# A fused S5 and Fourier network on one core: complex products summed by TensorE, the head's elementwise work on VectorE, the chunk scan as an up and a down sweep

## The chip, the cores and the metric

The kernel runs on one core of a Trainium2 chip. The metric is the device time of one execution in microseconds (us), as the median of several runs; lower is better. The change touches the first part of the program alone, its "head".

## The reference, cut to what matters

The program applies one adaptive-norm block with an S5 mixer and a squared-ReLU MLP to 256 latent tokens of 2048 channels, and then a block of two layers (convolution and spatial gating, Fourier mixing, two gated FFNs), all in fp32. The head computes the S5 mixer up to its Gelu: for each of 128 groups of 16 channels a complex state of 64 numbers goes over the 256 context tokens and then over the 256 latent ones, once forward and once backward in time, and the real part of C times the states is the output.

```python
def s5_discretise(a_re, a_im, log_dt, b_re, b_im):
    lam = lax.complex(a_re.astype(jnp.float32), a_im.astype(jnp.float32))
    dt = jnp.exp(log_dt.astype(jnp.float32))[:, None]
    lam_bar = jnp.exp(lam * dt)
    b = lax.complex(b_re.astype(jnp.float32), b_im.astype(jnp.float32))
    b_bar = ((lam_bar - 1) / lam)[..., None] * b
    return lam_bar, b_bar

def s5_scan(u, lam_bar, b_bar, s0, reverse):
    bu = jnp.einsum('btgh,gph->btgp', u, b_bar)
    first = -1 if reverse else 0
    bu = bu.at[:, first].add(lam_bar * s0)
    a = jnp.broadcast_to(lam_bar, bu.shape)
    _, states = lax.associative_scan(_lin_rec_combine, (a, bu), axis=1, reverse=reverse)
    return states
...
    for direction in range(2):
...
        st_ctx = s5_scan(uc_ctx, lam_bar, b_bar, s0, reverse)
        s_ctx_final = st_ctx[:, 0] if reverse else st_ctx[:, -1]
        st_lat = s5_scan(uc_lat, lam_bar, b_bar, s_ctx_final, reverse)
        y_lat = y_lat + jnp.einsum('btgp,ghp->btgh', st_lat, c_mat).real
```

## The kernel before, in words

**The tiling.** The 256 tokens of each stream are cut into 32 chunks of 8 (`L = 8`, `NC_ = 32`). The 128 groups are cut into four batches of 32 (`NB = 4`, `GB = 32`), and a batch's work into steps of four groups. The partitions hold the 64 states of both directions (2 x 64), or 8 tokens times 16 channels. PW, Q, R and WP hold powers of the discretised eigenvalue: Q those that carry a token to the end of its chunk, R those that carry a chunk's first state to its tokens, WP the powers 8, 16, 32, 64 and 128 for the scan over chunks.

**The stages of a batch** are generators in `s5_batch`, one `yield` for each step:

- `m`, `modulate()`: B is loaded; Bx (difference and sum of B's two parts) and qd (difference of Q's two parts) are made, on GpSimd but for batch 0; GpSimd multiplies the inputs u by their rstd rs; VectorE applies shift and scale to u. These come from `mod_matmul`, whose weights go through SP's queue of transfers.
- `e`, `inputs()`: eight steps. In each, `build` (L390 to L407) makes X, the complex product of Q's powers and B, by three products and two additions of 128x512 elements: the first product, tX, belongs to the real and to the imaginary part and is added to both. TensorE transposes X's eight 128x128 blocks (recorded at L69) into two PSUM banks, ScalarE copies them to W1 (L469), TensorE multiplies W1 by u (L476, 16 matmuls of 64 rows and 64 columns), and ScalarE copies the result into EC (context) and EL (latent), four copies of 64 partitions each (L484 and L485), in reversed order for the backward direction.
- `s`, `scan()`: the end states of the context's 32 chunks are summed in a tree of five levels (EC, at most four states in an instruction); the result is copied to EL[:, 0] (L525); then a loop over the 31 later chunks makes EL's states one after the other. One update is `mac`, L512 to L515: two products and two additions of 64 elements for each state.
- `z`, `outputs()`: eight steps. `build` makes Z, the conjugate powers R times C, in the same way; ScalarE copies B into bm (L557); TensorE makes the kernel of each group within a chunk from bm and Z (L562, and L566 for the diagonal); ScalarE copies it to Kp (L569) and issues four transfers that lay it out as the Toeplitz tile W4 (L573); ScalarE copies the states into SN (L576 and L577); `product`, two steps later (`ZLAG`), multiplies SN by Z and u by W4 into one bank (L545) and applies Gelu (L547). After the eight steps come transposes and the casts to high and low parts, z (L595 on ScalarE, L596 on VectorE).

**Which engine.** The tables X_ENG, Z_ENG and TREE (L34 to L38) give each step's `build` and each batch's tree to VectorE ('v') or GpSimd ('p'): of the 32 X, VectorE makes 24, of the 32 Z two, of the four trees three. X and Z of GpSimd lie in slots of tag Z, X of VectorE in slots of tag X.

**What sets the order.** ORDER (L44) is a list by hand: "m0:1" is one step of batch 0's modulation, "e2+z0:4" four steps each of batch 2's chunk inputs and batch 0's outputs in turn, and it ends in "s2 e3+z1 s3 z2 z3". Within each e step some modulation matmuls of a later batch are put (MODS), within z steps some of `mod_vectors` (WORK). The whole head stands in `tc.block(schedule_with_timeline_sim=True)`, whose scheduler then places the instructions on each engine. PSUM has four banks of tag ps (transposes and chunk inputs), two of py (kernels and products) and two of ab (modulation) in the head. Behind it is the dense part, products with weights from DRAM (`Dense.block`, first matmul line L648).

Of the kernel before, what the change touches and what calls it, by code (L numbers as in the profile page):

```python
# [18 lines left out]
P = 128  # L19
# [3 lines left out]
G = 128  # L23
# [95 lines left out]
def rstd_of(nc, pool, out, ssq, n, eps, shape, nm):  # L119
    """out = (ssq / n + eps) ** -0.5, with one Newton step."""  # L120
# [10 lines left out]
def cmul(eng, tmp, out, a, b):  # L131
    """out = a * b; re and im on axis -2 of out and b; a = (re, im) views without that axis."""
# [9 lines left out]
def head(k, raw, ctx):  # L142
# [8 lines left out]
    Q = hq.tile([P, 2, L, G], F32, name="Q")  # L151
# [8 lines left out]
    with ExitStack() as bx:  # L160
# [5 lines left out]
        sp = b2.tile([P, 3, GB, 16], F32, tag="C", name="sp").rearrange("p a b c -> p (a b c)").rearrange("p (n g) -> p n g", g=G)  # L166
# [17 lines left out]
        for b in range(NB):  # L184
            for i in range(2):
                u = uT[b][:, i]
                nc.sync.dma_start(u, a["xu"][:, b, i])
                sq = b3.tile([P, 2, 4, L * 16], F32, tag="X", name=f"xq{b}_{i}", bufs=XBUFS).rearrange("p a b c -> p (a b c)")
# [37 lines left out]
        for ri in range(2):  # L226
            S.copy(Q[0:64, ri, 1:8], PW[0:64, 7:0:-1, ri])
            S.copy(Q[0:64, ri, 0], WP[0:64, 0, ri])
            S.copy(Q[64:128, ri, 0:7], PW[64:128, 1:8, ri])
            S.copy(Q[64:128, ri, 7], WP[64:128, 0, ri])  # L230

        bms = []
        for i in range(2):
            bm = pools[0].tile([P, 2, 9, 16], F32, name=f"bm{i}")
# [58 lines left out]
def mod_vectors(k, raw, pool, st, vecs):  # L293
    """Column layout of the modulation vectors 2 to 5 for the latent stream, a step of 128 rows at a time."""
# [27 lines left out]
class ModVectors:  # L322
    """Modulation vectors 3 and 5 of the latent stream, feature by feature: sums over w_mod's columns times silu(c)."""
# [8 lines left out]
    def steps(self, raw, v):  # L332
        """One step for each 128 features and half of the rows."""
# [16 lines left out]
def mod_matmul(k, raw, b, st, acc):  # L350
    """Shift and scale of 512 channels before the bias, [(vector, half of the rows, stream), channels], in eight steps for each part."""
# [25 lines left out]
def s5_batch(k, pools, act, za, b, rs, ub, Q, R, WP, dd, bms, acc, ahead, work):  # L377
    """The stages of 32 groups: modulation, chunk inputs, scan, outputs; each is a generator of its steps."""
# [7 lines left out]
    def outer(p, m, jh):  # L386
        """Views of powers [p, j, g] and of m [p, g, h], over (g, j, h) or (g, h, j)."""
        shp = [P, 4, L, 16] if jh else [P, 4, 16, L]
        return (p.rearrange("p j g -> p g j").unsqueeze(3 if jh else 2).broadcast_to(shp),
                m.unsqueeze(2 if jh else 3).broadcast_to(shp))  # L390

    def build(tag, s, pw, pd, m, conj, jh):
        """Powers times m (or their conjugates) for four groups, with three products: the first belongs to both parts."""
        c = (Z_ENG if conj else X_ENG)[b][s]
        e = Pl if c == "p" else V
        slot = "Z" if conj or c == "p" else "X"
        out = b3.tile([P, 2, 4, L * 16], F32, tag=slot, name=f"{tag}{b}_{s}", bufs=ZBUFS if slot == "Z" else XBUFS)
# [92 lines left out]
    def scan():  # L490
# [36 lines left out]
        for c in range(1, NC_):  # L527
            mac(V, EL[:, c : c + 1], EL[:, c - 1 : c], 0, 1)
            if c % 4 == 3:
                yield  # L530
# [884 lines left out]
```

## Time and profile before

| | before |
|---|---|
| median of 3 runs | 3508.19 us (3506.8 to 3509.62) |
| the profiled execution: span, which is also all that the page times of it | 3504.0 us |
| TensorE, matmuls (PE), busy | 3164.2 us, 90% |
| TensorE, weight loads (PEld), busy | 3010.3 us, 86% |
| VectorE (DVE), busy | 2224.0 us, 63% |
| ScalarE (ACT), busy | 1474.4 us, 42% |
| GpSimd (POOL), busy | 556.2 us, 16% |

The profile is of one execution; its times are in us from the start of the span, and busy time leaves out branches, semaphores and the issue of transfers. A share of the whole span is a mean over the head and the dense part, so the stretches of the head are read by themselves: as slices of a fortieth of the span each, as windows with the busy time of each engine, as groups of instructions by line and shape, and as single instructions in order of time.

### The profile page before, as it was taken

The numbers are of one execution on the slowest core, as the hardware profiler recorded it, in microseconds if no ns is written. First come the engines' busy times: TensorE is split into PE (matmuls) and PEld (weight loads), VectorE is DVE, ScalarE is ACT, GpSimd is POOL, SyncE is SP. The second block draws the span as 40 slices with busy tenths as digits, with TensorE's granted clock in tenths as the row PEclk, the third lists the DMA queues.
The fourth block names the chain that finished last, engine by engine and source line by source line (L and its number), as shares of the span: only waits on it lengthen the run. The fifth ranks groups of instructions, "written<-read, shape, count | busy, mean of one in ns | idle before, by whom it ended". The sixth has DMA issues, their size and how long they took to land.

```text
span 3504.0 us, 66511 instructions
## 1 busy us (share of the span) xinstructions
PE 3164.2 (90%) x28206; PEld 3010.3 (86%) x28206; DVE 2224.0 (63%) x2936; ACT 1474.4 (42%) x1817; POOL 556.2 (16%) x368
## 2 busy tenths in 40 slices
PE   4655635998999999989999999999999999999998
PEld 1333325998999999988899999999999999999998
DVE  8999993678556554568855555554556555555455
ACT  2435424554444444443554433433444443343343
POOL 5756563011000000027710000000000000000000
PEclk7887756999999999999999999999999999999999
DMA  6664515784777766645555656666654665666664
GB/s 213 219 202 134 157 25 160 259 264 148 236 235 232 227 188 187 187 151 162 162 161 178 186 187 184 190 187 187 187 169 139 177 187 188 187 185 190 187 187 140
DMA packets 353530, 641.80 MB, mean 183 GB/s; under 512 B 23120, under 2 KB 92496, under 8 KB 352848
## 3 DMA queue, kind: packets, MB, share of 16 engines
q1 hardware_dynamic: 331824, 620.19, 56.9%
q10 hardware_dynamic: 21408, 17.36, 2.2%
q8 instruction: 220, 3.60, 0.4%
q14 instruction: 78, 0.64, 0.0%
HBM read 626.96 MB, written 2.10 MB: 180 GB/s over the span
## 4 chain that ended last, share of the span: by engine, by line
PE 52%; DVE 1%; issue 0%; ACT 0%; POOL 0%; DVEq 0%; ACTq 0%; POOLq 0%
PE ps L648 50%; PE ps L663 1%; PE ps L1260 0%; POOL wl L620 0%; PE ps L737 0%; PE ps L1285 0%; DVE xT L1234 0%; PE ps L750 0%; PE ps L1044 0%; PE ps L1121 0%; DVE pq L1277 0%; PE ps L1039 0%; PE ps L69 0%; DVE fl L1298 0%; DVE wl L620 0%
## 5 line engine op out<-in xcount | busy, mean ns | idle before, releaser
L620 DVE TENSOR_TENSOR wl<-wr,wh 128x1024 fp32r<-128x1024 f32 x907 | 1116.0, 1233 | 1028.4 <-ACT wh L619 1028.0
L619 ACT CAST wh<-wr 128x1024 fp32r<-128x1024 f32 x976 | 1022.7, 1049 | 1498.6 <-PE ps L648 1376.2
L648 PE MATMUL ps<-f,wh 128*128 128x256 f32 x5632 | 995.7, 279 | 0.0
L648 PEld LDWEIGHTS ps<-f,wh 128*128 128x128 f32 x5632 | 860.0, 188 | 0.1
L648 PE MATMUL ps<-f,wl 128*128 128x256 f32 x2816 | 787.6, 280 | 0.0
L648 PEld LDWEIGHTS ps<-f,wl 128*128 128x128 f32 x2816 | 527.9, 187 | 0.0
L648 PE MATMUL ps<-m,wh 128*128 128x256 f32 x2048 | 366.4, 281 | 8.8 <-DVE m L930 5.7
L648 PE MATMUL ps<-hd,wh 128*128 128x256 f32 x2048 | 360.6, 280 | 0.0
L648 PEld LDWEIGHTS ps<-m,wh 128*128 128x128 f32 x2048 | 315.0, 188 | 10.9 <-DVE m L930 6.9
L648 PEld LDWEIGHTS ps<-hd,wh 128*128 128x128 f32 x2048 | 312.6, 188 | 0.0
L648 PE MATMUL ps<-m,wl 128*128 128x256 f32 x1024 | 287.3, 281 | 0.0
L648 PE MATMUL ps<-hd,wl 128*128 128x256 f32 x1024 | 286.5, 280 | 0.0
L648 PE MATMUL ps<-f1d,wh 128*128 128x256 f32 x1408 | 248.9, 280 | 0.0
L648 PE MATMUL ps<-f0d,wh 128*128 128x256 f32 x1408 | 247.9, 280 | 0.0
L648 PEld LDWEIGHTS ps<-f1d,wh 128*128 128x128 f32 x1408 | 215.1, 188 | 0.0
L648 PEld LDWEIGHTS ps<-f0d,wh 128*128 128x128 f32 x1408 | 215.0, 188 | 0.0
L648 PE MATMUL ps<-f1d,wl 128*128 128x256 f32 x704 | 197.1, 280 | 0.0
L648 PE MATMUL ps<-f0d,wl 128*128 128x256 f32 x704 | 196.9, 280 | 0.0
L648 PE MATMUL ps<-z,wh 128*128 128x256 f32 x1024 | 184.5, 282 | 9.8 <-ACT wh L619 9.8
L648 PEld LDWEIGHTS ps<-m,wl 128*128 128x128 f32 x1024 | 193.3, 189 | 0.0
L648 PEld LDWEIGHTS ps<-hd,wl 128*128 128x128 f32 x1024 | 192.5, 188 | 0.0
L620 POOL TENSOR_TENSOR wl<-wr,wh 128x1024 fp32r<-128x1024 f32 x69 | 167.7, 2440 | 113.5 <-ACT wh L619 107.7
(491 smaller groups left out, 4730.2 us busy)
## 6 DMA issues: line engine op xcount, KB each, us to landing
wr<-in_ffn_w_gate_dram SPq DMA_DIRECT2D x176, 512.0 KB, 3.7
wr<-in_ffn_w_up_dram SPq DMA_DIRECT2D x176, 512.0 KB, 3.7
wr<-in_ffn_w_down_dram SPq DMA_DIRECT2D x176, 512.0 KB, 3.7
wr<-in_w_mlp_in_dram SPq DMA_DIRECT2D x128, 512.0 KB, 3.9
wr<-in_w_mlp_out_dram SPq DMA_DIRECT2D x128, 512.0 KB, 3.9
wv<-in_w_mod_dram SPq DMA_DIRECT2D x64, 512.0 KB, 5.0
wr<-in_s_w_glu_dram SPq DMA_DIRECT2D x64, 512.0 KB, 5.2
wv<-in_w_modt_dram SPq DMA_DIRECT2D x64, 512.0 KB, 4.4
```

Source lines behind the costliest of these rows:

```text
L619: nc.scalar.copy(hi, t)
L620: self.low(n).tensor_tensor(lo, t, hi.bitcast(F32), op=ALU.subtract)
L648: nc.tensor.matmul(o, lhsT=w[:, nt * P : (nt + 1) * P], rhs=x, start=(kt == 0 and nt % 2 == 0 and i == 0), stop=(kt == nk - 1 and nt % 2 = ...
L663: nc.tensor.matmul(acc[tt], lhsT=x[:, tk], rhs=w, start=(kt == 0 and i == 0), stop=(kt == nk - 1 and i == 2))
```

## The change: what it does

1. **X and Z are three products each, and nothing is added on an engine for elementwise work.** X is a list of three tiles (Q's real part times Bx, Q's imaginary part times the sum, qd times B's imaginary part), Z one of three parts. All products are VectorE's; X_ENG, Z_ENG and TREE go. TensorE does the additions, by accumulating in PSUM: 12 transposes in an X step instead of 8, into three banks; 24 chunk-input matmuls instead of 16, the eight of the common product with u broadcast to both parts, 128 columns wide; three parts of B in bm and of Z in the kernel instead of two; five terms in `product` instead of three.
2. **The scan is an up sweep of EC, the copy, an up sweep of EL and a down sweep of EL,** all on VectorE, with up to eight states in an instruction: 17 updates a batch (seven of eight states, two of seven, two of four, one of three, two of two, three of one) instead of the tree and 31 single updates.
3. **The rest of the head's GpSimd work moves to VectorE:** u times rs, Bx (one difference; the sum goes into B's new third part), qd and the sums of C. GpSimd keeps the memsets.
4. **Layouts and buffers.** Q has the eight powers of a group side by side, [2, G, L]; X has five buffers of one product each, W1 four buffers, three of which a step fills; u is read backward by the matmul for the backward direction, so that the copies into EC and EL cover all 128 partitions, two a step instead of four; C is loaded in halves, by eight transfers, and its sums and rd are made in `outputs()` instead of `scan()`.

The diff, cut to its core:

```diff
-X_ENG = ("vpvvpvvp", "ppvpvpvv", "vvvvvvvv", "vvpvvvvv")
-Z_ENG = ("pppppppp", "pppppppp", "pvpppppp", "ppppvppp")
-TREE = "vpvv"
-XBUFS, ZBUFS = 3, 4
+XBUFS, ZBUFS = 5, 4
...
-    Q = hq.tile([P, 2, L, G], F32, name="Q")
+    Q = hq.tile([P, 2, G, L], F32, name="Q")
...
-    def build(tag, s, pw, pd, m, conj, jh):
...
-        for o, p, i in ((tmp, pd[:, :, gl], 0), (out[:, 0], pw[:, 0, :, gs], 1), (out[:, 1], pw[:, 1, :, gs], 2)):
-            x, y = outer(p, m[i][:, gl], jh)
-            e.tensor_tensor(o.rearrange("p g (a c) -> p g a c", a=L if jh else 16), x, y, op=ALU.mult)
-        for i in range(2):
-            e.tensor_tensor(out[:, i], out[:, i], tmp, op=ALU.add)
+    def build(tag, s, pw, pd, m, conj):
+        if conj:
+            z = b3.tile([P, 3, 4, L * 16], F32, tag=tag, name=f"{tag}{b}_{s}", bufs=ZBUFS)
+            out = [z[:, t] for t in range(3)]
+        else:
+            out = [b3.tile([P, 4, L * 16], F32, tag=tag, name=f"{tag}{b}_{s}_{t}", bufs=XBUFS) for t in range(3)]
...
+        for t, mt in enumerate(m):
+            if conj:
+                p = pd[:, :, gl] if t == 2 else pw[:, t, :, gs]
+                x, y = p.rearrange("p j g -> p g j").unsqueeze(3), mt[:, 4 * (s % 4) : 4 * (s % 4) + 4].unsqueeze(2)
+            else:
+                p = pd[:, gl] if t == 2 else pw[:, t, gs]
+                x, y = p.unsqueeze(2), mt[:, gl].unsqueeze(3)
+            V.tensor_tensor(out[t].rearrange("p g (a c) -> p g a c", a=shp[2]), x.broadcast_to(shp),
+                            y.broadcast_to(shp), op=ALU.mult)
         return out
...
-            Pl.tensor_tensor(u, u, rs[:, i].unsqueeze(1).broadcast_to([P, GB, NC_]), op=ALU.mult)
+            V.tensor_tensor(u, u, rs[:, i].unsqueeze(1).broadcast_to([P, GB, NC_]), op=ALU.mult)
...
-            for hf in range(2):
+            for t in range(3):
                 ps = k.ps()
-                for gi in range(2):
-                    for ri in range(2):
-                        k.transpose(ps[:, (gi * 2 + ri) * P : (gi * 2 + ri + 1) * P], X[:, ri, 2 * hf + gi])
-                S.copy(W1[:, 2 * hf : 2 * hf + 2].rearrange("p g r q -> p (g r q)"), ps)
+                for g in range(4):
+                    k.transpose(ps[:, g * P : (g + 1) * P], X[t][:, g])
+                w = b3.tile([P, 4, P], F32, tag="W1", name=f"W1{b}_{s}_{t}", bufs=4)
+                S.copy(w.rearrange("p g q -> p (g q)"), ps)
+                W1.append(w)
...
+                    u = ub[:, :, 4 * s + g, ::-1] if d else ub[:, :, 4 * s + g]
+                    TE.matmul(pv[rows, g], lhsT=W1[2][:, g, rows], rhs=u.unsqueeze(1).broadcast_to([P, 2, 2, NC_]),
+                              start=True, stop=False, tile_position=(0, 64 * d))
+                    for ri in range(2):
+                        TE.matmul(pv[rows, g, ri], lhsT=W1[ri][:, g, rows], rhs=u, start=False, stop=(ri == 1),
+                                  tile_position=(0, 64 * d))
...
-        for c in range(1, NC_):
-            mac(V, EL[:, c : c + 1], EL[:, c - 1 : c], 0, 1)
+        yield from up(EL)
+        for lvl in range(3, -1, -1):
+            h = 1 << lvl
+            n = NC_ // (2 * h) - 1
+            v = EL[:, 2 * h - 1 : 2 * h - 1 + 2 * h * n].rearrange("p (n two h) r g -> p n two h r g", two=2, h=h)
+            mac(v[:, :, 1, 0], v[:, :, 0, 0], lvl)
+            yield
...
-            for t in range(3):
+            for t in range(5):
                 for q in range(4):
-                    if t < 2:
-                        lt, rh = SN[:, t, q], Z[:, t, q]
+                    if t < 4:
+                        lt, rh = SN[:, t % 2, q], Z[min(t, 2)][:, q]
...
-            for ri in range(2):
+            for ri in range(3):
```

How it moves the instructions on the engines, in three places. First VectorE, in the scan of batch 3, from the copy of the context's last state on. EC3 and EL3 are the states of context and latent stream, t1 and t2 the two products of an update. Before:

```order
L525 COPY EL3_2992<-EC3_2991 128x64
L512 TENSOR_TENSOR t1_3_10_4278<-EL3_2992,WP_89 128x64
L513 TENSOR_TENSOR t2_3_10_4279<-EL3_2992,WP_89 128x64
L514 TENSOR_TENSOR EL3_2992<-EL3_2992,t1_3_10_4278 128x64
L515 TENSOR_TENSOR EL3_2992<-EL3_2992,t2_3_10_4279 128x64
```

And in the change:

```order
L518 COPY EL3_3171<-EC3_3170 128x64
L503 TENSOR_TENSOR t1_3_7_4539<-EL3_3171,WP_89 128x512
L504 TENSOR_TENSOR t2_3_7_4540<-EL3_3171,WP_89 128x512
L505 TENSOR_TENSOR EL3_3171<-EL3_3171,t1_3_7_4539 128x8x64
L506 TENSOR_TENSOR EL3_3171<-EL3_3171,t2_3_7_4540 128x8x64
```

Behind the copy stood 31 updates of one state each, and stand now the sweeps' updates of up to eight states.

Second VectorE, at the end of the head: Z2 and Z3 are the outputs' operands of batches 2 and 3, C2 and C3 their C, rd3 a difference of powers. Before, the last scan ends here:

```order
L512 TENSOR_TENSOR t1_3_40_4458<-EL3_2992,WP_89 128x64
L513 TENSOR_TENSOR t2_3_40_4459<-EL3_2992,WP_89 128x64
L514 TENSOR_TENSOR EL3_2992<-EL3_2992,t1_3_40_4458 128x64
L515 TENSOR_TENSOR EL3_2992<-EL3_2992,t2_3_40_4459 128x64
L403 TENSOR_TENSOR Z3_4_5195<-R_88,C3_4217 128x512 x2
L405 TENSOR_TENSOR Z3_4_5195<-Z3_4_5195,tZ3_4_5196 128x512 x2
L596 TENSOR_TENSOR z3_5481<-py191_5471,z3_5481 128x4x128
```

And in the change:

```order
L504 TENSOR_TENSOR t2_3_17_4600<-EL3_3171,WP_89 128x448
L505 TENSOR_TENSOR EL3_3171<-EL3_3171,t1_3_17_4599 128x7x64
L506 TENSOR_TENSOR EL3_3171<-EL3_3171,t2_3_17_4600 128x7x64
L403 TENSOR_TENSOR Z2_7_5124<-R_88,C2_1_4725 128x512 x2
L403 TENSOR_TENSOR Z2_7_5124<-rd2_4605,C2_1_4725 128x512
L533 SCALAR_TENSOR_TENSOR rd3_5262<-R_88 128x256
L539 TENSOR_TENSOR C3_1_5382<-C3_1_5382 128x256
L540 TENSOR_TENSOR C3_1_5382<-C3_1_5382 128x256
L403 TENSOR_TENSOR Z3_0_5268<-R_88,C3_0_5264 128x512 x2
L403 TENSOR_TENSOR Z3_0_5268<-rd3_5262,C3_0_5264 128x512
```

Scan 3 now ends among the outputs of batch 2, ahead of Z2's last step, and all of Z3 follows on VectorE.

Third TensorE, in an X step of batch 2 (step 3): X2_3 is the operand that is transposed into ps, W12_3 its copy, ab the modulation sums, py and Z0 the outputs of batch 0. Before:

```order
L69 MATMUL ps81_2064<-ident_58,X2_3_2056 128x128 x4
L305 MATMUL ab71_1783<-wv2_8_0_2566,st_91 32x512 x2
L305 MATMUL ab71_1783<-wv2_8_1_2570,st_91 32x512 x2
L69 MATMUL ps82_2070<-ident_58,X2_3_2056 128x128 x4
L305 MATMUL ab71_1783<-wv2_9_0_2574,st_91 32x512 x2
L476 MATMUL ps83_2076<-u2_85,W12_3_2063 64x64 x16
```

And in the change:

```order
L66 MATMUL ps101_2217<-ident_58,X2_3_1_2205 128x128 x4
L552 MATMUL py133_3111<-Z0_6_2858,SN0_6_2912 32x128 x4
L552 MATMUL py133_3111<-W40_6_2907,u0_83 32x128 x4
L66 MATMUL ps102_2224<-ident_58,X2_3_2_2206 128x128 x4
L475 MATMUL ps103_2231<-u2_85,W12_3_2_2229 64x128
L478 MATMUL ps103_2231<-u2_85,W12_3_0_2215 64x64
L478 MATMUL ps103_2231<-u2_85,W12_3_1_2222 64x64
```

The step now takes three banks for transposes and a fourth for the chunk inputs, whose matmuls are interleaved part by part, and outputs of batch 0 stand between the transposes.

## Rows read from the trace of the kernel before

**Rows 1.** The page's slices: VectorE's busy tenths and TensorE's granted clock.

```profile
DVE  8999993678556554568855555554556555555455
...
PEclk7887756999999999999999999999999999999999
```

**Rows 2.** Windows: us, busy PE, PEld, DVE, ACT, POOL; clock, DMA share, GB/s.

```profile
0.00:589.20 589.20, 316.86 (x4580) 192.71 (x4580) 511.03 (x981) 221.13 (x435) 343.44 (x258) 0.74 0.50 153
41.00:470.00 429.00, 241.83 (x3432) 144.94 (x3432) 408.00 (x716) 164.27 (x331) 270.54 (x195) 0.76 0.51 161
470.00:537.00 67.00, 25.21 (x536) 19.73 (x536) 64.69 (x143) 16.87 (x39) 45.02 (x38) 0.54 0.16 23
537.00:589.00 52.00, 23.54 (x512) 19.09 (x512) 6.03 (x12) 23.73 (x46) 16.05 (x14) 0.62 0.55 132
```

**Rows 3.** Timeline of TensorE: start, duration, instruction, what it waited for.

```profile
589.22 0.79 PE L648 MATMUL ps<-z,wh 128*128 128x256 f32 x2 [9.79 <-ACT wh L619]
```

**Rows 4.** Timeline of VectorE at several places of the head.

```profile
81.06 1.97 DVE L403 TENSOR_TENSOR X<-Q,Bx 128x512 f32<-128x512 f32 x2
...
500.39 1.14 DVE L513 TENSOR_TENSOR t<-EL,WP 128x64 f32<-128x64 f32 x1
...
520.57 0.23 DVE L512 TENSOR_TENSOR t<-EL,WP 128x64 f32<-128x64 f32 x1
520.71 0.22 DVE L513 TENSOR_TENSOR t<-EL,WP 128x64 f32<-128x64 f32 x1
...
521.35 0.23 DVE L512 TENSOR_TENSOR t<-EL,WP 128x64 f32<-128x64 f32 x1
...
540.72 1.29 DVE L403 TENSOR_TENSOR Z<-R,C 128x512 f32<-128x512 f32 x2 [3.49 <-PE py L545]
541.93 1.28 DVE L405 TENSOR_TENSOR Z<-Z,tZ 128x512 f32<-128x512 f32 x2
```

**Rows 5.** VectorE's groups by form, 0 to 600 us: busy, mean ns; idle before.

```profile
L403 DVE TENSOR_TENSOR X<-Q,Bx 128x512 f32<-128x512 f32 x48 | 69.1, 1481 | 11.8 <-PE ps L69 5.9 <-POOL Bx L415 3.5 <-ACT Q L230 2.4
L515 DVE TENSOR_TENSOR EL<-EL,t 128x64 f32<-128x64 f32 x124 | 48.3, 389 | 3.4
L405 DVE TENSOR_TENSOR X<-X,tX 128x512 f32<-128x512 f32 x48 | 45.9, 996 | 0.0
L403 DVE TENSOR_TENSOR tX<-qd,B 128x512 f32<-128x512 f32 x24 | 29.8, 1241 | 0.0
L514 DVE TENSOR_TENSOR EC<-EC,t 128x256 f32<-128x256 f32 x21 | 20.3, 968 | 0.0
```

**Rows 6.** Windows of TensorE alone: lines L562, L545, transposes of X, L476.

```profile
41.00:589.00 548.00, 58.84 (x1536) 46.32 (x1536) 0.72 0.47 141
41.00:589.00 548.00, 42.57 (x768) 27.88 (x768) 0.72 0.47 141
41.00:589.00 548.00, 46.51 (x256) 0.72 0.47 141
41.00:589.00 548.00, 43.80 (x1024) 37.44 (x1024) 0.72 0.47 141
```

**Rows 7.** TensorE, kernel products: timeline, and the windows around them.

```profile
456.10 2.04 PE L562 MATMUL py<-Z,bm 128*32 128x128 f32 x48 [15.99 <-DVE EL L514]
...
563.84 1.15 PE L562 MATMUL py<-Z,bm 128*32 128x128 f32 x48 [0.64 <-POOL Z L405]
...
456.00:460.00 4.00, 3.90 (x116) 3.94 (x120) 3.76 (x18) 0.95 (x3) 0.00 (x0) 0.50 0.00 0
563.60:568.00 4.40, 2.06 (x80) 1.73 (x80) 0.00 (x0) 1.76 (x5) 0.25 (x1) 1.00 0.52 78
```

**Rows 8.** Timeline of ScalarE: Gelus of the last steps.

```profile
556.53 0.28 ACT L547 ACTIVATE u<-py 128x128 f32<-128x128 f32 x1 [3.00 <-DMA W<-Kp]
...
561.73 0.28 ACT L547 ACTIVATE u<-py 128x128 f32<-128x128 f32 x1 [2.59 <-PE py L566]
...
571.00 0.45 ACT L547 ACTIVATE u<-py 128x128 f32<-128x128 f32 x2 [2.76 <-issue]
```

More of the change, by code (lines that the diff above doesn't have):

```diff
@@ L500, in scan, with mac @@
         cnt = [0]
-        def mac(e, out, prev, lvl, n):
+        def mac(out, prev, lvl):
+            n = out.shape[1]
+            if n > 8:
+                for i in range(0, n, 8):
+                    mac(out[:, i : min(i + 8, n)], prev[:, i : min(i + 8, n)], lvl)
+                return
             shp = [P, n, 2, GB]
             cnt[0] += 1
-            if e is Pl:
-                t = b1.tile([P, 4, L * 16], F32, tag="tmpp", name=f"t_{b}_{cnt[0]}")
-                t1, t2 = (v.rearrange("p a (r g) -> p (a r) g", g=GB).rearrange("p (a r) g -> p a r g", r=2)[:, :n]
-                          for v in (t[:, 0:2], t[:, 2:4]))
-            else:
-                t1, t2 = (b1.tile([P, 4, 2, GB], F32, tag=f"t{i}", name=f"t{i}_{b}_{cnt[0]}")[:, :n] for i in (1, 2))
-            e.tensor_tensor(t1, prev, wr[:, lvl].unsqueeze(1).unsqueeze(1).broadcast_to(shp), op=ALU.mult)
-            e.tensor_tensor(t2, prev[:, :, ::-1, :], wx[:, lvl].unsqueeze(1).broadcast_to(shp), op=ALU.mult)
-            e.tensor_tensor(out, out, t1, op=ALU.add)
-            e.tensor_tensor(out, out, t2, op=ALU.add)
@@ L517, in scan @@
-        cur = EC
-        for lvl in range(5):
-            pr = cur.rearrange("p (n two) r g -> p n two r g", two=2)
-            n = 16 >> lvl
-            for i in range(0, n, 4):
-                m = min(n, 4)
-                mac(Pl if TREE[b] == "p" else V, pr[:, i : i + m, 1], pr[:, i : i + m, 0], lvl, m)
-            cur = pr[:, :, 1]
-        V.tensor_copy(EL[:, 0], EC[:, NC_ - 1])
-        yield
-        for c in range(1, NC_):
-            mac(V, EL[:, c : c + 1], EL[:, c - 1 : c], 0, 1)
-            if c % 4 == 3:
-                yield
+            t1, t2 = (b1.tile([P, 8, 2, GB], F32, tag=f"t{i}", name=f"t{i}_{b}_{cnt[0]}")[:, :n] for i in (1, 2))
@@ new lines, in mac, with up @@
+            V.tensor_tensor(t1, prev, wr[:, lvl].unsqueeze(1).unsqueeze(1).broadcast_to(shp), op=ALU.mult)
+            V.tensor_tensor(t2, prev[:, :, ::-1, :], wx[:, lvl].unsqueeze(1).broadcast_to(shp), op=ALU.mult)
+            V.tensor_tensor(out, out, t1, op=ALU.add)
+            V.tensor_tensor(out, out, t2, op=ALU.add)
+        def up(E):
+            cur = E
+            for lvl in range(5):
+                pr = cur.rearrange("p (n two) r g -> p n two r g", two=2)
+                mac(pr[:, :, 1], pr[:, :, 0], lvl)
+                cur = pr[:, :, 1]
+                yield
@@ L532, in outputs @@
+        yield from up(EC)
+        V.tensor_copy(EL[:, 0], EC[:, NC_ - 1])
+        yield from up(EL)
[4 more added lines that the diff above has]
+            mac(v[:, :, 1, 0], v[:, :, 0, 0], lvl)
+            yield
     def outputs():
@@ L551, in outputs @@
             gg = b * GB + gl
-            Z = build("Z", s, R, tl["rd"], [tl["C"][:, i] for i in range(3)], True, True)
+            if s == 2:
+                load_c(1)
+            Z = build("Z", s, R, rd, [Cs[s // 4][:, i] for i in (1, 2, 0)], True)
             bm = bms[s % 2]
@@ L556, in outputs @@
                 rows = slice(64 * d, 64 * d + 64)
-                S.copy(bv[rows, :, :, d, :], Bt[rows, 0:2, gl : gl + 4, :])
+                S.copy(bv[rows, :, :, d, :], Bt[rows, :, gl : gl + 4, :])
             pk = k.ps("py")
-            for ri in range(2):
+            for ri in range(3):
                 for d, o, c in ((0, 112, slice(0, 128)), (1, 112, slice(112, 128)), (1, 0, slice(0, 112))):
@@ L563, in outputs @@
                                   lhsT=bm[:, ri, 2 * q + d : 2 * q + d + 2, :].rearrange("p d h -> p (d h)"),
-                                  rhs=Z[:, ri, q, c], start=(ri + d == 0), stop=False, tile_position=(0, 32 * q))
+                                  rhs=Z[ri][:, q, c], start=(ri + d == 0), stop=False, tile_position=(0, 32 * q))
             for q in range(4):
```

80 lines of the change are left out of this document (35 added, 45 removed).

## Prediction

> **What bounds the kernel now.** I read the page's slices first, 87.6 us each: VectorE is 8 to 9 tenths busy throughout the first six (525 us) and nowhere else for so long, and the granted TensorE clock is under full in the first seven alone [rows 1]. The first matmul of the dense part starts at 589.22 us [rows 3]; the change touches nothing behind it, so the 3504.0 - 589.2 = 2914.8 us after it stay. The stretches come next [rows 2]: from 41 to 470 us VectorE works 408 of 429 us, from 470 to 537 us 65 of 67, while TensorE works 242 and 25; from 537 to 589 us no engine is full, which is the tail of the last batch's outputs. VectorE bounds the head up to 537 us, and 52 us of latency close it.
>
> Why it is so busy is in its rows. The same 128x64 instruction takes 1.14 us while GpSimd runs tensor instructions, and 0.22 us after GpSimd's queue has run dry; then one state's four instructions go by in 521.35 - 520.57 = 0.78 us [rows 4]. The groups carry the mixture: 124 of the 128x64 additions at 0.39 us, 128x512 additions at 1.00 us and products at 1.48 and 1.24 us [rows 5], against 1.21 us for two products (541.93 - 540.72) with GpSimd idle [rows 4]. I take the length of the slow ones as waiting for GpSimd.
>
> **The change, part by part: VectorE.** Its busy time up to 589 us is 511 us [rows 2].
> - Scan. The serial recurrence goes: four lines of 124 instructions, 48.3 us for the last [rows 5], which I take for each: 193 us. The tree's 128x256 instructions go, on VectorE for three batches: four lines, taken at the 20.3 us of the row each, 81 us [rows 5]. In their place each batch has 17 updates of four instructions: 7 of eight states, 2 of seven, 2 of four, 1 of three, 2 of two, 3 of one. A 128x512 instruction at 0.60 us makes 2.4 us an update, one state 0.78 us [rows 4]; in between I go by size (2.1, 1.4, 1.1, 1.0): 16.8 + 4.2 + 2.8 + 1.1 + 2.0 + 2.3 = 29 us a batch, 117 us.
> - X and Z. VectorE's X work, 69.1 + 45.9 + 29.8 = 145 us [rows 5], goes; 64 steps of three products come, 192 x 0.60 = 115 us. The layout of Q now has the powers side by side. If that did not help, X's 96 products stay at the 0.98 us (half of 1.97) of the two at 81.06 us [rows 4], 96 x 0.38 = 36 us more; I take 0.60, the row of a product with a broadcast power.
> - From GpSimd: eight 128x1024 products by rs (1.2 us each by size, 10 us) and some 28 small ones for B, C and qd (11 us). GpSimd keeps only memsets in the head.
> Sum: 511 - 193 - 81 + 117 - 145 + 115 + 21 = 345 us, 381 at the high end; relief of the other slow instructions, such as those on u, is left out and would lower it.
>
> These prices are the distances between starts: in the quiet stretch the next instruction starts 0.14 us after the start of one that lasts 0.23 us (520.57 and 520.71) [rows 4]. The Trainium skill says otherwise (VectorE: DVE Perf Modes, The DRAIN you can't avoid): the next instruction cannot issue until the pipe is empty. By that rule full durations would add up, about 0.07 us on each of some 460 scan and product instructions, 32 us more; the starts in this trace contradict it, and the sum goes by them.
>
> **TensorE.** From 41 to 589 us the kernel products take 58.84 us, the output products 42.57, the transposes of X 46.51, the chunk inputs 43.80 [rows 6]. They grow to three parts from two (+29), to five terms from three (+28), to 12 transposes from 8 (+23), and to twice the columns (+44): 125 us, 317 to 442 us at the clock of now. The same 48 records of kernel products took 1.15 us at a granted clock of 1.00 (2.4 GHz) and 2.04 us at 0.50 (1.2 GHz), a ratio of 1.77 [rows 7]. At the mean clock of 0.72 to 0.74 [rows 2, 6] about half the time is at each level, so 442 us is some 342 us if all ran at 2.4 GHz and 605 us if all ran at 1.2 GHz.
>
> **ScalarE.** W1 copies grow from 64 to 96, and the 128 half-partition copies into EC and EL become 64: its sum falls a little. In the tail one output step takes 561.73 - 556.53 = 5.2 us there, with the four transfers that it issues [rows 8]; the third B part adds 0.1.
>
> **What ends last now.** VectorE no longer fills the head, so I follow two stretches. First, X steps with the outputs of batches 0 and 1, up to the last X step: TensorE has 46.51 x 1.5 + 43.80 x 2 = 157 us of X, half of (58.84 x 1.5 + 42.57 x 5/3) and a little for the diagonal, 85 us, and of the other 124 us (317 less the four rows) some 100 us: 342 us at the clock of now, 265 us at 2.4 GHz, 470 at 1.2. VectorE has about 230 us there and waits. The stretch with the largest share of TensorE, 242 of 429 us, has the highest mean clock, 0.76 against 0.54 and 0.62 [rows 2], so I expect no lower one; I take 305 us, the middle between 265 and 342. With 41 us of lead, 10 until the first X step is at TensorE, and 15 for the starts of batches, whose EC copies must wait for the tree of the batch before in its one buffer, the last X step is at 371 us.
> Second, the outputs of batches 2 and 3. The order puts ScalarE's first step of batch 2 behind the last X step; about 15 us remain of scan 2, then 16 steps at 5.4 us (5.2 as now, and a fuller TensorE), 86 us, and from the last Gelu at 571.00 to the dense part at 589.22 us 18 us as now [rows 3, 8]. Scan 3 is 29 us of VectorE and hides under batch 2's steps; if it did not, batch 3 would start up to 29 us late. 371 + 15 + 86 + 18 = 490 us instead of 589: 99 us less.
> The profiled execution's span becomes 3405 us. The page times no more than the span; the median of the runs is 4.2 us above it, and I keep that: 3409 us.
>
> **The rivals.**
> 1. TensorE keeps pace at 2.4 GHz, and VectorE or ScalarE sets the time. For: half of its time now it is granted the full clock at less work. Then the head is VectorE's 345 us and the 52 us of tail, 397 us: 3316 us. Against: both engines would have to mesh in their fixed orders almost without a wait.
> 2. Taking turns. There are four banks for X and the chunk inputs; a step now uses all four (before, three), and W1 has four buffers for three a step. TensorE then waits for ScalarE's copies in each of the 32 X steps, about one and a half copies of 512 columns more; at the 1.00 us of VectorE's additions of that size [rows 5], the nearest row, that is 1.5 us a step or 48 us: a head near 538 us, 3457 us. For: three of the four buffers are filled anew in every step. Against: the order puts modulation and output products between.
> 3. Slower: TensorE stays at 1.2 GHz and becomes the bound. The first stretch is then 41 + 10 + 15 + 470 = 536 us, and an output step goes by TensorE: (58.84 x 1.5 + 42.57 x 5/3) / 32 = 5.0 us at the clock of now [rows 6], 6.8 us (times 605/442) at 1.2 GHz. 15 + 16 x 6.8 + 18 = 142 follow: 678 us, 89 us slower, 3597 us. It decides once the first stretch needs over 404 us, that is when less than a third of the work is done at 2.4 GHz. For: 0.54 and 0.62 in the last stretches [rows 2]. Against: there TensorE was idle more than half the time, waiting for VectorE.
> 4. GpSimd is not the cause, and VectorE's instructions are slow by themselves; then 192 products stay near 1.36 us (the mean of 1.48 and 1.24) [rows 5], 146 us more, and the scan's at 0.39 to 0.22 times 117, 90 us more: 581 us of VectorE and the 52 us of tail, 44 us past the 589: 3552 us. The two prices of one instruction [rows 4] speak against it.
>
> **How the numbers follow.** Forecast as told, head 450 to 530 us: 0.67. Rival 1: 0.14. Rival 2: 0.12. Rival 3: 0.05. Rival 4: 0.01; 0.01 is left for no change. Within the forecast, 305 us may be 265 to 342, X may cost 36 us more on VectorE, and scan 3 up to 29 us: 3370 to 3450 us of its own. To leave out no more than 2 in 10, the range takes in rival 2 and half of rival 1: 3345 to 3475 us. Faster than by 0.2% (7 us, about what a measurement of this kernel can tell): 0.92, the forecast, both milder rivals less a hundredth; within 0.2%: 0.02; slower: 0.06.
>
> **What would show it.** Right: no tensor instruction of GpSimd before the dense part; 128x512 products of X and Z near 0.65 us each (0.60 between starts); VectorE's sum near 350 us and no longer full; TensorE's busy time over 360 us in a shorter head at a higher clock; the first dense matmul near 490 us; the dense part unchanged. Wrong: X products at 1.0 us; VectorE still over 90% busy; a granted clock under 0.65 with TensorE full; or a dense part of another length.

## The result, and the profile after

The changed kernel takes 3379.08 us (median of 4 runs, 3370.44 to 3385.47) against 3507.49 us for the kernel before in the same session: a ratio of 0.9636, 95% interval 0.9617 to 0.9656, some 128 us. The forecast was 3409 us, 99 us less than before, in a range of 3345 to 3475 us. The profiled execution's span is 3382.1 us.

The page's slices after (84.6 us each), which answer to [rows 1]:

```profile
DVE  8688736785565555689555545555556455555555
...
POOL 0000010110000000167300000000000000000000
PEclk9999779999999999989999999999999999999999
```

The windows after, columns as in [rows 2]: the head, the stretch in which X steps run, and the end of the head.

```profile
0.00:464.10 464.10, 369.49 (x6501) 262.05 (x6501) 335.70 (x742) 207.83 (x403) 1.20 (x7) 0.93 0.63 195
35.00:350.00 315.00, 281.05 (x4535) 197.30 (x4539) 253.29 (x527) 150.62 (x293) 0.00 (x0) 0.98 0.68 222
350.00:464.00 114.00, 65.55 (x1896) 56.08 (x1884) 54.77 (x109) 44.51 (x94) 0.00 (x0) 0.77 0.40 84
```

GpSimd is silent in the head but for 1.20 us of memsets, VectorE's sum is 335.70 us instead of 511.03, TensorE's is 369.49 instead of 316.86, and its granted clock has risen from 0.74 to 0.93, to 0.98 in the long stretch. The dense part starts at 464.10 us instead of 589.22 (timeline of TensorE, as [rows 3]):

```profile
464.10 0.80 PE L657 MATMUL ps<-z,wh 128*128 128x256 f32 x2 [7.57 <-ACT wh L628]
```

So the head is 125.1 us shorter; what follows takes 2918.0 us, 3.2 us more than before. (In the profiled executions of all versions below, what follows the head took between 2905 and 2919 us, although nothing in it was changed. A few us between two medians therefore say little by themselves, and the start of the dense part is given beside them.) VectorE's groups, which answer to [rows 5], and single instructions of the last scan, which answer to [rows 4]:

```profile
L403 DVE TENSOR_TENSOR Z<-R,C 128x512 f32<-128x512 f32 x64 | 41.3, 687 | 26.2 <-PE py L552 26.0
L403 DVE TENSOR_TENSOR X<-qd,B 128x512 f32<-128x512 f32 x32 | 22.1, 691 | 33.4 <-PE ps L66 33.1
...
L505 DVE TENSOR_TENSOR EL<-EL,t 128x512 f32<-128x512 f32 x16 | 11.0, 686 | 0.0
```

```profile
356.61 0.69 DVE L503 TENSOR_TENSOR t<-EL,WP 128x512 f32<-128x512 f32 x1
357.22 0.68 DVE L504 TENSOR_TENSOR t<-EL,WP 128x512 f32<-128x512 f32 x1
357.82 0.68 DVE L505 TENSOR_TENSOR EL<-EL,t 128x512 f32<-128x512 f32 x1
358.54 0.69 DVE L506 TENSOR_TENSOR EL<-EL,t 128x512 f32<-128x512 f32 x1
359.15 0.69 DVE L503 TENSOR_TENSOR t<-EL,WP 128x512 f32<-128x512 f32 x1
```

The 128x512 instructions of X, Z and the scan take 0.69 us, and VectorE now waits for TensorE (33.1 and 26.0 us). The scan's four lines, by their windows, are 34 us each, 136 us with overlaps counted twice. Among TensorE's waits from 30 to 464 us those for ScalarE's W1 copies are small (total, times, longest):

```profile
PE ps L475 <- ACT W L467: 7.4, 5, 3.5
```

Rows of ScalarE's timeline place the end of the X steps and the pace of the last outputs; between two Gelus lie four transfers that it issues in 3.27 us:

```profile
337.69 0.62 ACT L481 COPY EC<-ps 128x256 f32<-128x256 f32 x1 [3.54 <-DMA W<-Kp]
...
431.00 0.28 ACT L554 ACTIVATE u<-py 128x128 f32<-128x128 f32 x1 [3.33 <-DMA W<-Kp]
...
433.73 3.27 ACTq L582 DMA_DIRECT2D W<-Kp  x4
437.04 0.28 ACT L554 ACTIVATE u<-py 128x128 f32<-128x128 f32 x1 [3.34 <-DMA W<-Kp]
```

### The profile page after: what moved, and what is told of

It reads as the page before. It is cut to its first block, busy times and chain, and to the rows that moved or that the text cites. A ratio compares the mean times of both kernels' runs of the same rounds, so it can differ in the third digit from the quotient of the medians.

```text
span 3382.1 us, 69851 instructions
## 1 busy us (share of the span) xinstructions
PE 3217.1 (95%) x30126; PEld 3080.4 (91%) x30126; DVE 2049.5 (61%) x2699; ACT 1461.2 (43%) x1785; POOL 213.0 (6%) x117
## 4 chain that ended last, share of the span: by engine, by line
PE 54%; DVE 1%; issue 0%; ACT 0%; POOL 0%; DVEq 0%; ACTq 0%; POOLq 0%
PE ps L657 52%; PE ps L672 1%; PE ps L1269 0%; POOL wl L629 0%; PE ps L746 0%; DVE xT L1243 0%; PE ps L759 0%; PE ps L1294 0%; PE ps L1053 0%; PE ps L1130 0%; DVE pq L1286 0%; PE ps L1048 0%; PE ps L66 0%; DVE fl L1307 0%; DVE wl L629 0%
## 5 line engine op out<-in xcount | busy, mean ns | idle before, releaser
L629 DVE TENSOR_TENSOR wl<-wr,wh 128x1024 fp32r<-128x1024 f32 x907 | 1115.6, 1232 | 1022.8 <-ACT wh L628 1022.1
```

Of the source, the lines that this page charges most:

```text
L629: self.low(n).tensor_tensor(lo, t, hi.bitcast(F32), op=ALU.subtract)
```

## The experiments

The head was taken apart from both sides. Theory A is that of the prediction: VectorE was slow because GpSimd's tensor instructions ran beside it. Theory B: the arithmetic itself, above all the serial recurrence, was the cost. Theory C: the gain is TensorE's summing. All ratios are to the kernel before, run beside each.

**1. The kernel before with GpSimd's tensor work in the head given to VectorE, nothing else changed.**

```diff
-X_ENG = ("vpvvpvvp", "ppvpvpvv", "vvvvvvvv", "vvpvvvvv")
-Z_ENG = ("pppppppp", "pppppppp", "pvpppppp", "ppppvppp")
-TREE = "vpvv"
+X_ENG = ("vvvvvvvv",) * 4
+Z_ENG = ("vvvvvvvv",) * 4
+TREE = "vvvv"
...
-            Pl.tensor_tensor(u, u, rs[:, i].unsqueeze(1).broadcast_to([P, GB, NC_]), op=ALU.mult)
+            V.tensor_tensor(u, u, rs[:, i].unsqueeze(1).broadcast_to([P, GB, NC_]), op=ALU.mult)
```

(and in the same way qd, Bx and the sums of C)

> The kernel before, with all tensor instructions of the head that GpSimd had moved to VectorE, in the same form (three products and two additions for X and Z, tree and serial recurrence); nothing goes to TensorE and no sweep is made. Theory A (VectorE was slow because GpSimd ran beside it): VectorE's 128x512 instructions start 0.60 us apart and a state of the recurrence takes 0.78 us throughout, VectorE's sum is about 192 (X, Z) + 148 (scans) + 104 (the rest) = 444 us although it does much more, the dense part starts near 500 us, and the time is about 3420 us. Theory B (the amount of arithmetic on VectorE decides): 30 more Z and 8 more X on VectorE at today's prices are some 230 us more, the time is over 3600 us.

Measured: 3433.92 us, ratio 0.9794 (0.9777 to 0.9811), 70 us less. Windows of the head and its X stretch, then groups of VectorE:

```profile
0.00:526.00 526.00, 325.87 (x4580) 188.77 (x4580) 454.53 (x1232) 221.97 (x435) 0.96 (x7) 0.80 0.56 171
41.00:350.00 309.00, 220.83 (x2794) 115.23 (x2790) 291.34 (x700) 129.91 (x255) 0.00 (x0) 0.88 0.67 213
```

```profile
L403 DVE TENSOR_TENSOR X<-Q,Bx 128x512 f32<-128x512 f32 x64 | 64.4, 1043 | 12.5 <-PE ps L69 12.5
L405 DVE TENSOR_TENSOR X<-X,tX 128x512 f32<-128x512 f32 x64 | 41.5, 685 | 0.0
...
L515 DVE TENSOR_TENSOR EL<-EL,t 128x64 f32<-128x64 f32 x124 | 27.7, 223 | 3.3
```

VectorE executes 1232 instructions instead of 981, and is busy 56 us less: the recurrence's line falls from 389 to 223 ns, the additions from 996 to 685 [rows 5]. Theory A holds, B falls; the dense part starts at 526 us, 26 later than forecast, with VectorE 10 us over its 444. X's products stay at 1.04 us with nobody beside them; that part was Q's layout, not GpSimd (run 9 shows the same in the changed kernel).

**2. The changed kernel with tree (at most four states an instruction) and recurrence put back.**

```diff
-        yield from up(EL)
-        for lvl in range(3, -1, -1):
...
+        for c in range(1, NC_):
+            mac(EL[:, c : c + 1], EL[:, c - 1 : c], 0)
```

> The changed kernel with the tree (at most four states an instruction) and the serial recurrence of before put back; GpSimd stays quiet. Theory A: with GpSimd quiet a serial scan is 31 x 0.78 = 24 us and its tree 13 us, against 29 us for the sweeps; VectorE's sum grows by some 32 us to 368 us and has slack: 3379 to 3395 us. Theory B (the recurrence itself was the cost): the 185 us and more of the serial lines come back, 3450 us or more.

Measured: 3382.93 us, ratio 0.9659 (0.9636 to 0.9681), which overlaps the change's interval; the dense part starts at 467.81 us, 4 us later, and VectorE's sum is 347.20 us, 11.5 us over the change's (32 were forecast). The sweeps are worth next to nothing there. Theory B falls again.

**3. The kernel before with the sweeps,** `mac`, `up` and the loops of the change, in the place of tree and recurrence. One thing differs from the change: t1, the first product of an update, is put into the buffer that VectorE's tX and tZ use, of which there is one.

```diff
-                t1, t2 = (b1.tile([P, 4, 2, GB], F32, tag=f"t{i}", name=f"t{i}_{b}_{cnt[0]}")[:, :n] for i in (1, 2))
...
+            t1, t2 = (b1.tile([P, 4, L * 16], F32, tag=("tmpv", "t2")[i], name=f"t{i}_{b}_{cnt[0]}")
```

> The kernel before with the sweeps of the change in place of tree and recurrence, all four scans on VectorE; GpSimd keeps X, Z and the rest. Theory A: the sweeps' 128x512 instructions last 1.0 us and more beside GpSimd, a scan costs some 50 us instead of 68, VectorE's sum falls by about 70 us: 3430 to 3460 us. Theory B (the recurrence itself was the cost): instructions at 0.69 us, 29 us a scan, 157 us less of VectorE, near 3350 us.

Measured: 3508.84 us, ratio 1.002 (1.0008 to 1.0033): no gain at all, which neither theory expected. Windows, then waits of GpSimd's queue and of TensorE, then VectorE's timeline at the end of the last scan:

```profile
0.00:593.50 593.50, 319.24 (x4580) 191.18 (x4580) 457.31 (x649) 220.60 (x435) 329.49 (x222) 0.75 0.49 152
470.00:540.00 70.00, 28.25 (x661) 23.77 (x665) 25.39 (x55) 21.46 (x49) 41.72 (x37) 0.57 0.19 28
```

```profile
POOL Z L403 <- PE py L550: 147.8, 9, 68.8
POOL qd L413 <- DVE tX L403: 31.8, 1, 31.8
...
PE py L567 <- DVE Z L405: 36.3, 1, 36.3
```

```profile
490.86 0.62 DVE L516 TENSOR_TENSOR EL<-EL,t 128x448 f32<-128x448 f32 x1
491.40 0.68 DVE L403 TENSOR_TENSOR tZ<-rd,C 128x512 f32<-128x512 f32 x1
```

VectorE is relieved by 54 us (457.31 against 511.03) and is idle two thirds of the stretch from 470 to 540 us, which it filled before [rows 2]; there GpSimd, with its Z, is the busiest engine (41.72 of 70 us). Ahead of that GpSimd had stood 68.8 us before a Z until TensorE's products freed a buffer, but TensorE was itself waiting, 36.3 us, for a Z of VectorE, whose tZ starts right behind the last update of scan 3. At scan 2 it is the same: X's other products stand ready, and the first tX starts at 439.93 us, right behind the last update at 439.39. The shared buffer accounts for this order: a tX or tZ that follows a scan in the program has to wait for the scan's last t1. That is read from the kernel and these times, not shown by a run of its own. So this run doesn't price the sweeps by themselves, and what they are worth beside a working GpSimd is open.

**4 and 5. The changed kernel with X's sums, and with X's and Z's sums, on VectorE.** X lies here in two buffers of two parts, and its common product in one of its own. Of X (Z alike):

```diff
+        if not conj:
+            for t in range(2):
+                V.tensor_tensor(out[t], out[t], out[2], op=ALU.add)
...
-            for t in range(3):
+            for t in range(2):
                 ps = k.ps()
...
-                    TE.matmul(pv[rows, g], lhsT=W1[2][:, g, rows], rhs=u.unsqueeze(1).broadcast_to([P, 2, 2, NC_]),
-                              start=True, stop=False, tile_position=(0, 64 * d))
```

> The changed kernel with X summed by VectorE again (three products and two additions, 8 transposes, 16 chunk-input matmuls, two W1 copies a step); Z stays three products. Theory A (TensorE now bounds the stretch up to the last X step, VectorE has slack there): VectorE +64 x 0.60 = 38 us, TensorE -17 us of transposes and about -27 us of chunk inputs: the last X step comes up to 25 us sooner, 3355 to 3380 us. Theory C (the gain of the change came from TensorE taking the sums): at least the 38 us come back, 3410 us or more.

> The changed kernel with both X and Z summed by VectorE again (five instructions a step, 8 transposes, 16 chunk inputs, two parts of B, three output terms); sweeps, Q's layout and the quiet GpSimd stay. Theory A (GpSimd's silence gives most, and the rest is whatever brings VectorE's sum under TensorE's time): VectorE 336 + 64 x 2 x 0.60 = 413 us, TensorE some 45 us less than in the run with X's sums alone; VectorE fills the stretch up to the last X step again, the head grows by 10 to 35 us, the granted clock falls under 0.93: 3390 to 3415 us. Theory C (VectorE has room for 77 us, the products by TensorE are worth nothing): 3370 to 3385 us. Theory D (the gain beyond the quiet GpSimd is TensorE's summing alone): as the first run, 3425 us or more.

Measured: 3377.67 us, ratio 0.9634 (0.9615 to 0.9652), and 3404.58 us, ratio 0.9713 (0.9696 to 0.973). First the windows of X's sums alone, then those of both:

```profile
0.00:458.90 458.90, 336.95 (x5860) 206.37 (x5860) 371.05 (x808) 193.53 (x371) 1.20 (x7) 0.91 0.64 197
35.00:350.00 315.00, 258.16 (x4148) 149.24 (x4150) 290.26 (x592) 139.53 (x270) 0.00 (x0) 0.95 0.70 224
```

```profile
0.00:487.98 487.98, 333.35 (x4580) 192.63 (x4580) 409.70 (x872) 190.05 (x371) 1.21 (x7) 0.80 0.61 185
35.00:350.00 315.00, 242.86 (x3048) 128.00 (x3044) 279.17 (x563) 118.73 (x234) 0.00 (x0) 0.86 0.69 220
```

X's sums by TensorE gain nothing by themselves: VectorE has the 35 us (the dense part starts at 458.94 us, 5 us earlier). With Z's sums as well 26 us of the change's gain go: some 100 us of the 128 stay with GpSimd silent, the sweeps and the new layouts, 30 us more than in run 1. So theory C holds for 26 us. The extra work of TensorE cost no time in the change: 281, 258 and 243 us of its busy time in the same 315 us stand beside granted clocks of 0.98, 0.95 and 0.86.

**6. GpSimd given back 48 products,** Z of batches 0 and 1.

```diff
-            V.tensor_tensor(out[t].rearrange("p g (a c) -> p g a c", a=shp[2]), x.broadcast_to(shp),
+            (Pl if conj and b < 2 else V).tensor_tensor(out[t].rearrange("p g (a c) -> p g a c", a=shp[2]), x.broadcast_to(shp),
```

> The changed kernel with the 48 products of Z of batches 0 and 1 on GpSimd, everything else as in the change. Theory A: while GpSimd works, VectorE's 128x512 instructions last 1.0 to 1.4 us instead of 0.69, so that VectorE's sum does not fall by the 48 x 0.60 = 29 us it gives away but stays or grows; the time is 10 to 50 us more, 3390 to 3430 us. Rival (GpSimd is a free helper, and the scheduler's order was the matter before): VectorE's instructions stay at 0.69 us and the time at 3365 to 3385 us.

Measured: 3394.59 us, ratio 0.9685 (0.9669 to 0.9701), some 15 us more than the change. The head's window, and the timelines of VectorE and GpSimd while GpSimd multiplies:

```profile
0.00:478.63 478.63, 373.70 (x6500) 267.16 (x6500) 341.38 (x696) 208.43 (x403) 66.73 (x55) 0.91 0.62 189
```

```profile
249.05 1.19 DVE L504 TENSOR_TENSOR t<-EL,WP 128x128 f32<-128x128 f32 x1
250.16 1.19 DVE L505 TENSOR_TENSOR EL<-EL,t 128x128 f32<-128x128 f32 x1
...
250.05 1.15 POOL L403 TENSOR_TENSOR Z<-rd,C 128x512 f32<-128x512 f32 x1
```

The same shape in the change:

```profile
354.74 0.28 DVE L504 TENSOR_TENSOR t<-EC,WP 128x128 f32<-128x128 f32 x1
```

VectorE has 46 instructions fewer in the head and a sum 6 us larger: a 128x128 instruction of 0.28 us takes 1.19 us there. The helper costs more than it takes over. That GpSimd's own Z came too late is not in the waits: TensorE waits 0.8 us for it in all, but 11.1 us (0.8 in the change) for VectorE's smg, a step of the modulation. The last X step's copy begins 13.5 us later than in the change, about the 15 us. Theory A, shown in the changed kernel too.

**7 and 8. W4's transfers off ScalarE's queue,** onto SP's for batches 2 and 3, or onto GpSimd's for all.

```diff
-                nc.scalar.dma_start(W4[:, q, :], bass.AP(v.tensor, v.offset, [v.ap[0], [-16, L], [1, P]]))
+                nc.gpsimd.dma_start(W4[:, q, :], bass.AP(v.tensor, v.offset, [v.ap[0], [-16, L], [1, P]]))
```

> The changed kernel with the four transfers of W4 of each step of batches 2 and 3 issued on SP's queue instead of ScalarE's. If ScalarE's own time sets the 125 us from the last X step to the dense part, its 2.5 to 3.3 us of issuing a step go, 16 times: the stretch falls by 25 to 45 us and the time to 3335 to 3355 us. If the chain of a step (kernel, copy, transfer, product) sets it, the time stays within 10 us of the change.

> The changed kernel with the four transfers of W4 of every step issued on GpSimd's queue, which is otherwise idle, instead of ScalarE's. If ScalarE's issuing sets the end: also 16 times 2.5 to 3.3 us, and something in the first stretch: 3325 to 3350 us. If GpSimd's issue of a transfer is slower than 1 us each, the products wait for W4 and the time stays or grows; if GpSimd's issuing disturbs VectorE as its tensor instructions do, VectorE's 0.69 us grow.

Measured: 3355.39 us, ratio 0.9576 (0.9559 to 0.9593), and 3353.05 us, ratio 0.9564 (0.9546 to 0.9582). Timeline of ScalarE with GpSimd's queue, two Gelus of the last batch:

```profile
407.16 0.28 ACT L554 ACTIVATE u<-py 128x128 f32<-128x128 f32 x1
...
410.99 0.28 ACT L554 ACTIVATE u<-py 128x128 f32<-128x128 f32 x1
```

Timeline of GpSimd's queue, and a group of VectorE:

```profile
406.06 2.08 POOL L582 DMA_DIRECT2D W<-Kp  x4 [0.51 <-ACT Kp L578]
```

```profile
L403 DVE TENSOR_TENSOR X<-qd,B 128x512 f32<-128x512 f32 x32 | 22.0, 689 | 27.2 <-PE ps L66 27.0
```

A step is 3.8 us instead of 6.0. From the copy of the last X step to the dense part it is 106 us in both versions (337.94 to 443.83 us in run 7, 328.04 to 433.79 in run 8) instead of 126. So ScalarE's issuing, which the prediction had within its 5.4 us a step, cost some 20 us of the end of the head; 25 to 45 were forecast, and both medians lie just above their forecast ranges. In run 8 the X steps also end 10 us sooner; the transfers of batches 0 and 1, which run 7 leaves on ScalarE, are the difference between the two. VectorE's instructions stay at 0.69 us: GpSimd issuing transfers does not disturb them, its tensor instructions do.

**9. The changed kernel with Q's old layout,** `Q = hq.tile([P, 2, L, G], F32, name="Q")` and the views to match.

> The changed kernel with Q laid out as before, the powers of a group 128 elements apart instead of side by side. The run without GpSimd showed X's products at 1.04 us with that layout and 0.69 us for the rest, so X's 96 products take 96 x 0.35 = 34 us more on VectorE, 370 us in all. Theory A (VectorE has slack in the changed kernel): the time stays within 10 us of the change, 3370 to 3390 us, as it did with 35 us more for X's sums. Theory E (X's build is in the chain of each step): 32 x 1.05 us or some 34 us more, 3405 to 3415 us.

Measured: 3393.4 us, ratio 0.9675 (0.9647 to 0.9703), between the two forecasts; the interval just touches the change's. X's products take 1.05 us, VectorE's sum is 368 us, 32 us more, and the dense part starts 8 us later. By that or by the 14 us of the medians, more than half of the 32 us is hidden.

**10 and 12. The sweeps where VectorE is full:** run 1 with the sweeps added (with the shared buffer of run 3), and run 5 with the serial scan of run 2.

> The kernel before with all of GpSimd's tensor work on VectorE (as the first run, 3434 us) and the sweeps as well. Theory A (where VectorE is the bound, what it is spared counts): the scans' 164 us of the first run become 136 us as in the change, VectorE's sum falls from 454 to about 427 us and the time by 15 to 30 us, 3405 to 3420 us; the sweeps, worth nothing beside a working GpSimd and nothing in the change, are worth this much in between. Rival (the sweeps never matter): 3428 to 3440 us.

> The changed kernel with X's and Z's sums on VectorE (3405 us by itself) and with the tree and the serial recurrence of before as well; Q's layout, the copies over all partitions and the quiet GpSimd stay. VectorE is nearly full here. Theory A (a scan counts by its time on VectorE where VectorE is full): 164 us of scans instead of 136, the head 15 to 30 us longer, 3420 to 3435 us. Theory F (what the sweeps spare on VectorE is lost in the order of the stages, as the run of before with all on VectorE and sweeps suggests, which was 33 us slower than the same with the serial scan): 3375 to 3410 us.

Measured: 3466.97 us, ratio 0.9884 (0.9856 to 0.9911), 33 us slower than run 1; and 3417.18 us, ratio 0.9742 (0.9714 to 0.977), 13 us slower than run 5 and between the two forecasts; the intervals of runs 5 and 12 overlap, and the dense part starts 12 us later. Head of run 10, head of run 12:

```profile
0.00:551.70 551.70, 340.27 (x4580) 189.01 (x4580) 454.31 (x864) 221.37 (x435) 0.96 (x7) 0.79 0.54 163
```

```profile
0.00:500.22 500.22, 326.83 (x4580) 188.88 (x4580) 422.45 (x1240) 189.80 (x371) 1.21 (x7) 0.80 0.59 180
```

Both forecasts rested on 28 us of VectorE, the difference of the scans' durations added up (164 and 136 us); that counts the overlap of one instruction with the next twice, and the short ones overlap most (0.22 us long, 0.14 apart [rows 4]). The sums of the windows say 12.8 us (422.45 against 409.70) and nothing (454.31 against 454.53). The first agrees with the 12 and 13 us of run 12; why the sum does not fall in run 10 is open. Run 10 was slower than either theory had it. Its waits name two places, TensorE behind X of batch 3 and behind the first Z of batch 2:

```profile
PE ps L69 <- DVE X L405: 32.8, 5, 19.7
PE py L567 <- DVE Z L405: 32.8, 1, 32.8
```

Both are the shared buffer's order again. On VectorE's timeline the first tX of batch 3 starts at 373.00 us, right behind the last update of scan 2 (372.46), and the first tZ of batch 2 at 443.71 us, right behind that of scan 3 (443.17). In run 1, where the updates have buffers of their own, tZ stands between the updates of scan 3 (419.51, 424.53). That accounts for the last X step, 17 us later than in run 1, and for the end of the head; no run gave the sweeps buffers of their own in the kernel before. So the 33 us are no price of the sweeps, and runs 2 and 12 are the ones that price them.

**11. W4 on GpSimd's queue and X's sums on VectorE together.**

> The changed kernel with W4's transfers on GpSimd's queue (3353 us by itself) and X's sums on VectorE again (3378 us by itself, against 3379). If the two act in different stretches, X's sums let the last X step come some 10 us sooner, and the end is the shorter one: 3335 to 3353 us. If VectorE with its 35 us more has become the bound once ScalarE's issuing is gone: 3355 to 3375 us.

Measured: 3357.11 us, ratio 0.9574 (0.9551 to 0.9598), no better than run 8 and in the second forecast's range. Its last X step begins its copy at 328.31 us, as in run 8 (328.04), so X's sums on VectorE bring it no sooner here; the dense part starts 8 us later, but the profiled execution is the slowest of run 11 and the fastest of run 8. Run 8 has the lowest median; the intervals of runs 7, 8 and 11 overlap.

## Why the prediction was right, and what it mis-sized

- **VectorE bound the head, and GpSimd beside it was why.** Run 1 alone gives 70 of the 128 us with more work on VectorE, run 6 takes some back. In the kernel before, the length of the instructions changes where GpSimd's last product of a run ends (514.63 + 1.10 us). Rival 4 is out.

```profile
514.63 1.10 POOL L403 TENSOR_TENSOR tZ<-rd,C 128x512 f32<-128x512 f32 x1
514.80 1.01 DVE L515 TENSOR_TENSOR EL<-EL,t 128x64 f32<-128x64 f32 x1
515.84 0.23 DVE L512 TENSOR_TENSOR t<-EL,WP 128x64 f32<-128x64 f32 x1
```

- **VectorE's sum** was forecast at 345 us and is 335.70; products at 0.69 us, starts 0.60 us apart.
- **The scan term had about the right total and the wrong cause.** I took 193 + 81 us away and put 117 in their place, 157 us net, as the price of the form; the four lines of VectorE summed to 279 us before and sum to 136 now, 143 us less. The total came out because the change removes both causes at once. Runs 2 and 12 show that the old form costs only 12 us more once GpSimd is silent: nearly all of the term belongs to GpSimd. The row with 0.78 us for a state [rows 4], from which 31 x 0.78 = 24 us for a serial scan follows, was in the prediction and would have told this.
- **The layout of Q** was rightly taken at 0.60 us a product; my upper bound (0.98 us, 36 us in all) is what runs 1 and 9 show for the old layout (1.04 us, 32 us), so that bound was no risk of the change but a part of its gain, and more than half hidden.
- **TensorE.** "I take 305 us, the middle between 265 and 342" is the mis-sized term. The last X step was forecast at 371 us and comes at 338: the granted clock went to 0.98, not to the middle, so the stretch is near the 265 us end (338 less 41, 10 and 15 leaves 272). The row I had, 0.76 in the fullest stretch [rows 2], pointed that way; runs 4 and 5 and the change put clock and filling of the same 315 us in one order (0.86, 0.95, 0.98 for 243, 258 and 281 us).
- **The end of the head** was forecast at 15 + 86 + 18 = 119 us and is 464 - 339 = 125, with ScalarE's steps at 5.2 to 6.0 us; runs 7 and 8 show that its issuing of transfers takes about 20 us of it. The Gelu at 571.00 us, from which the 18 us were taken, was not the last one; the row below is. As the changed kernel has the same last Gelu behind its double one (447.03 us), the term held: 17 us from there to the dense part.

```profile
577.13 0.28 ACT L547 ACTIVATE u<-py 128x128 f32<-128x128 f32 x1 [5.69 <-PE py L545]
```

- **The sum:** 26 us sooner in the head than forecast, 3 us later in the dense part, and a median 3 us under the span where I had added 4.2: together the 30 us between 3409 and 3379.
- **The rivals.** Taking turns (48 us): TensorE waits 7.4 us for W1's copies from 30 us to the end of the head, and X's sums on VectorE, with two W1 copies instead of three, gain nothing in time (run 4). TensorE at 1.2 GHz: the clock rose. TensorE at full clock with VectorE or ScalarE setting the time (3316 us) came half true: the clock is there, but the engines do not mesh without waits, 59 us of VectorE's for TensorE alone in the two rows above.
- **TensorE's summing** was taken as a load that the clock decides about. Run 5 prices it: 26 us gained for both sums. Which of the two fullest engines ends last in the X stretch is not settled: run 4 gave VectorE 37 us more there and took 23 us from TensorE, and the last X step came 11 us sooner.

## What to carry to other kernels

Price an engine's work with its neighbour silent before rewriting it: here one row of a quiet stretch (0.22 against 1.14 us for one instruction) held more of the gain than any change of the algorithm, and the rewritten scan was worth 13 us at most once the neighbour was gone. After a bound is removed the parts of a change do not add up: 70 us for silence, next to nothing for the sweeps and for X's sums alone, 26 for both sums. When a part is put into the old kernel by itself, see that it shares no buffer there that it has for itself in the new one. And an engine that issues its own transfers pays for them in its steps; look for an idle queue.

## What the runs showed of the hardware that was not expected

- An independent 128x512 instruction starts 0.60 us after the one before (356.61, 357.22, 357.82), but one that reads what the one before wrote starts 0.72 us after it (357.82, 358.54): its whole duration of 0.69 us and a little. An update is 2.54 us, not 2.4. The prediction weighed the rule of the Trainium skill (VectorE: DVE Perf Modes, The DRAIN you can't avoid) that the next instruction does not start until the pipe is empty, and left out that the section goes on to say that one which is not held starts earlier. The starts 0.60 us apart agree with the exception. Whether the 0.72 us is the pipe or the wait for a result, no run here tells apart.
- A product of 128x512 whose powers lie 128 elements (512 bytes) apart, or 32 for qd, takes 1.04 to 1.05 us, with the powers side by side 0.69 us, GpSimd being silent in both (runs 1 and 9). The Trainium skill (SBUF — State Buffer, Door 1: The DMA port swizzle) says that each access to a new line of 16 bytes pays a penalty; the trace agrees in direction. Z's power, which steps as far but is repeated 16 times in the innermost loop, stays at 0.69 us.
- GpSimd's queue issues a transfer in about 0.52 us (2.08 us for four) and does not slow VectorE, whose 128x512 instructions stay at 0.69 us (run 8); GpSimd's tensor instructions do, to 1.19 us from 0.28 for one of 128x128 (run 6).
- TensorE did more work in the head in less time at a higher granted clock: 0.74 with 317 us busy of 589 in the head before, 0.80 with 333 of 488 in run 5, 0.91 with 337 of 459 in run 4, 0.93 with 369 of 464 after. No run varied one of these alone.
